# Four value products moved to later visits, a bias tile padded from 16 to 64 columns, four decay sums moved one block on

## The chip, the core and the metric

One core of a Trainium2 chip runs one launch of the kernel. The metric is the device time of a run in microseconds. The kernel before took 982.14, 982.09 and 980.04 us in three runs, so its median is 982.09 us.

## The reference, cut to what matters

Two layers on a sequence of 256 tokens with a model width of 2048. The first is a Mamba-2 mixer (8 groups, 64 heads of 64), the second a sliding-window attention with 32 query heads in 4 groups of 8, each group on one key/value head. Each layer ends in a layer norm. The part that the change touches most is the attention of one group and its output projection:

```python
s = jnp.einsum("bcqhrd,bckhd->bchrqk", qb, kk).astype(jnp.float32) * (hd ** -0.5)
s = jnp.where(valid[None, :, None, None], s, -jnp.inf)
...
p = jnp.exp(s - m)
p = p / (jnp.sum(p, axis=-1, keepdims=True) + jnp.exp(sk - m))
o = jnp.einsum("bchrqk,bckhd->bcqhrd", p.astype(vv.dtype), vv)
...
o = o * jax.nn.silu(gate)
return o @ w_out
```

In the Mamba layer, each head needs a 128 x 128 decay factor per chunk, the exponential of a difference of running sums, which the kernel makes on ScalarE.

## The kernel before, in words

**Products.** Every large matrix is kept in two halves: a rounded high part (`wh`, `xH`, `yH`, `x1H`, `oH`) and the rest (`wl`, `xL`, `yL`, `x1L`, `oL`), and each product is three matmuls, high by high, low by high and high by low. Weights arrive in units of 128 x 2048 numbers (two DMAs of 512 KB on the SP queue into `wr`). ScalarE makes the high half (L164), VectorE the low one (L167), two units ahead of their use. A unit then feeds TensorE in one of two forms:
- 48 matmuls of 128 x 256 (L252, in `mac`), with the weights stationary and the activations moving: the input projections of the first layer (`xH`, `xL`), and the query and gate projections of the second (`x1H`, `x1L`).
- 24 matmuls of 128 x 512 (L323 to L325, in `out_unit`), with the activations stationary and the weights moving: the output projections, from `yH`, `yL` in the first layer and from `oH`, `oL` in the second. The kernel has 8 groups of them in the first layer and 4 in the second.

**Visits.** Between units, TensorE makes short visits to small plain float32 products, which write PSUM tiles named `ax`: in the first layer the chunk products, in the second the scores (L1160 for the first 128 tokens, L1167 for the second) and the value products (L1270 for the first 128 tokens; L1284 and L1291 for the second).

**The second layer's clock.** The order of its units is `B_ORDER`: q0 g0 q1 g1 q2 o0 g2 q3 o1 g3 o2, each of four units, and o3 at the very end by `out_last`. A call to `tick()` stands behind every unit. `later(n, fn)` puts a piece of work into a list, and the n-th tick from there runs it; within a tick, pieces run in the order in which they were put in. For group j, `attend(j, 0)` (scores and softmax of the first half) runs three ticks behind the last query unit; it puts in `pv` of that half `PV_AT[j][0]` ticks on, and `attend(j, 1)` three ticks on, which puts in its own `pv` `PV_AT[j][1]` ticks on. `pv` multiplies by the values on TensorE, gates the result into `o` on VectorE (L1258), and splits it into `oH` (ScalarE, L1298) and `oL` (VectorE, L1299). Instructions of an engine stand in the order that the tile framework gives them; an engine runs them in that order.

**Tiles in memory.** The second layer's tiles come from the pool `bp`, laid one behind another in the order in which their tags first appear: `snk` (64 columns of 4 bytes), `rot`, `kT`, `vt`, `qT`, `qb`, and behind `qb` the tags `pt0`, `pri`, `gb0`, `gb1`, `qt`, `rt`, `p`, `sg`, `sm`, `own`, `ze`, `oH`, `oL` and some small ones. `qb` has 16 columns of 4 bytes, 64 bytes; every tile ahead of it has a multiple of 256 bytes. So in the built program `kT`, `vt` and `qT` start on a multiple of 256 bytes, and everything behind `qb`, `oH` (byte 161600) and `oL` (169792) among it, starts 64 bytes past one. The weight tiles, `yH`, `yL`, `x1H` and `x1L` start on multiples of 256. A unit of the query and gate projections lies 64 bytes into its weight tile (`BROKEN`), one of the output projections at its start (`WHOLE`).

**The first group.** `sum_decay(0, 0, ...)` makes the eight ScalarE instructions of the first half group's decay sums (L550), in two parts of four. They read `rb`, a copy of running sums that are written to memory and read back by a DMA. The first part is planned behind block 5 of the first layer (`halves[0][0]`), the second behind block 6. `beside[k]` instead puts a function into block k's convolution (`conv_silu`, L492 to L500), behind its ScalarE and VectorE scaling and ahead of its tanh.

Of the kernel before, what the change touches and what calls it, by code (L numbers as in the profile page):

```python
# [8 lines left out]
F32 = mybir.dt.float32  # L9
# [5 lines left out]
ALU = mybir.AluOpType  # L15
AX = mybir.AxisListType

P = 128
# [43 lines left out]

MOVE_AT = [[2, 3, 3, 4], [3, 4, 5, 6]]
MOVE_LAST = [2, 3, 3, 4]
PV_AT = [[6, 7], [6, 7], [8, 7], [7, 5]]
RES_AT = [2, 2, 3, 3, 4, 5, 5, 6]
ALPHA = (2.0 * 2) ** 0.25
NEG = -1.0e30
# [15 lines left out]
def trunk(ctx: ExitStack, tc: tile.TileContext, A: dict, out: bass.AP, dbg=None):  # L84
    nc = tc.nc
    PSUM = bass.MemoryType.PSUM

    def pool(name, bufs=1, side=None, space=None, stack=ctx):
        kw = {"space": space} if space is not None else {}
        return stack.enter_context(  # L90
            tc.tile_pool(name=name, bufs=bufs, side=side, reuse_waits="tile", **kw)
        )
# [165 lines left out]
    def later(n, fn, place=None):  # L258
        pending.insert(len(pending) if place is None else place, [n, fn])
# [562 lines left out]
    beside = {}  # L822
# [6 lines left out]
    def at(t, fn, *a):  # L829
        plan.setdefault(t, []).append((fn, *a))  # L830
# [5 lines left out]
    for g in range(NG):  # L836
        t = 10 * g
        if g == 0:
            at(TD, turn_dt, *dts)
            at(4, load_decay, 0, 1)  # L840
            at(8, load_low, 0)
            pos = dict(cb=CB0, y=13)

            between[11] = [(turn_first, 0)]
            halves = [(5, 6, 7), (7, 8, 9)]
            by = (9, 10)
        elif g == 1:
            at(10, load_decay, 1, 0)
            at(10, load_decay, 1, 1)
            at(15, load_low, 1)  # L850
            pos = dict(cb=6, y=Y_AT, norm=10 + CB_AT)

            halves = [(13, 14, 15), (15, 16, 16)]
            by = (16, 17)
        else:
            at(t - 5, load_decay, g, 0)
            at(t - 5, load_decay, g, 1)
            at(t, load_low, g)
            pos = dict(cb=CB_AT, y=Y_AT, norm=10 + CB_AT)
        for hf in range(2):  # L860
            if g < 2:
                sa, sb, ex = halves[hf]
                if (g, hf) != (1, 0):
                    at(sa, sum_decay, g, hf, 0, 2)
                at(sb, sum_decay, g, hf, 2, 4)
                at(ex, exp_decay, g, hf)
            else:
                for i in range(2):
                    beside[t + 3 * hf + i] = sum_decay, g, hf, 2 * i, 2 * i + 2
                beside[t + 3 * hf + 2] = exp_decay, g, hf  # L870
        if g == 1:
            at(16, norm, 0)
        at(t + pos["cb"], cb, g)
        for hf in range(2):
            at(by[hf] if g < 2 else t + pos["cb"] + hf, by_cb, g, hf)
        if g > 0:
            xs_at = t + 6
            if g == 1:
                between[17] = [(turn_xs, 1)]
            else:  # L880
                at(xs_at, turn_xs, g)
            for n, js in enumerate(((0, 1), (2, 3))):
                at(xs_at + n + (g == 1), carry_xs, g, js)
            at(xs_at + 2, scale_xs, g)
        at(t + pos["y"], ymm, g)
        if g == 0:
            at(t + pos["y"], sum_decay, 1, 0, 0, 2)
        for i in range(4):
            at(t + pos["y"], gate, g, i)
        if g > 0:  # L890
            at(t + pos["norm"], norm, g)
# [88 lines left out]
    bp = pool("bp")  # L980
# [56 lines left out]
    vt = bp.tile([P, 2, S], F32, tag="vt", name="vt")  # L1037
    kvb = bp.tile([P, 512], F32, tag="qT", name="kvb", bufs=2)
    nc.gpsimd.dma_start(kvb[:], A["kvb"].partition_broadcast(P))
    qb = bp.tile([P, 16], F32, tag="qb", name="qb")  # L1040
    nc.gpsimd.dma_start(qb[:], A["qb"])
    kv_u = []
    for h in range(2):
        ps = mm_tile()
# [36 lines left out]

    def rope_maps():

        nc.gpsimd.tensor_scalar(qb[:], qb[:], 0.125, None, ALU.mult)
        z = bp.tile([P, 2, 2, 32], F32, tag="rt", name="z", bufs=1)
        nc.vector.transpose(z[:].rearrange("p h m t -> p (h m t)"), turned[:].rearrange("p h m t -> p (h m t)"))
        for k in range(2):
            lo = 64 * k
            for a in range(4):
                nc.scalar.copy(  # L1090
                    rot[lo : lo + 32].rearrange("p m (h a t) -> p a m h t", h=2, a=4)[:, a],
                    z[32 * a : 32 * a + 32].rearrange("p h m t -> p m h t"),
                )

    later(1, rope_maps)
    swap = [*range(8, 16), *range(8), *range(16, 32)]

# [42 lines left out]
    def attend(j, h):  # L1140
# [161 lines left out]
        turn_far()  # L1302
        later(PV_AT[j][h], pv)
        if h == 0:
# [202 lines left out]
```

## Time and profile before

| what | value |
|---|---|
| three runs | 982.14, 982.09, 980.04 us |
| the profiled execution's own time | 980.68 us |
| its span, first to last instruction | 978.6 us |
| outside the span | 980.68 - 978.6 = 2.1 us |
| granted TensorE clock, mean | 0.999 |
| first layer, roughly | 0 to 651 us |
| second layer, roughly | 651 us to the end; query, gate and output units from 680 us |

The profile's page lists busy time per engine, then the chain of work that ended last, then groups of instructions. A group's row reads: line, engine, operation, output<-inputs, shapes, count, then busy us, mean ns of one, and the idle time ahead of them. In a timeline row the first column is the start, the second the length, both in us. A matmul's length is partly modelled and matmuls overlap, so the pace of a stream is the distance of starts, not the length. In the chain, a row is start, length, and what ran; "x144" says that 144 instructions are in it.

### The profile page before, as it was taken

Reading aid. Unit: us, or ns where it says so; the run is one execution under the profiler, and the core shown is the slowest. Engines: PE = TensorE matmul, PEld = TensorE weight load, DVE = VectorE, ACT = ScalarE, POOL = GpSimd, SP = SyncE. Lnnn points to the kernel's source line nnn. Section 1 sums busy time; section 2 is a strip of 40 time slices with the busy share of each in tenths; the row PEclk is TensorE's granted clock in tenths of the full one; section 3 lists DMA queues with packets and bytes.
Section 4 is the critical chain, followed back from the end, with each engine's and each line's share of the span. In section 5 each row is a group of like instructions: output and inputs, shape, how many; then the busy total and the mean of one; then the engine's idle time right before and its main releaser. Section 6 shows DMA issues by size and latency. Waiting matters only on the chain.

```text
span 978.6 us, 18818 instructions
## 1 busy us (share of the span) xinstructions
PE 972.5 (99%) x7364; PEld 896.7 (92%) x7364; DVE 789.4 (81%) x1202; ACT 666.5 (68%) x1254; POOL 103.2 (11%) x145
## 2 busy tenths in 40 slices
PE   9999999999999999999999999999999999999997
PEld 8999989999999998999999999888999988988976
DVE  7888898976888877885887787889977778778786
ACT  7585885864985865776576487467567776784762
POOL 0000303004003001200300300412000000000003
PEclk9999999999999999999999999999999999999999
DMA  9788567755665766666666566458654645465632
GB/s 357 251 284 326 160 210 235 249 201 152 207 218 190 250 208 199 212 200 206 191 205 201 171 211 198 148 187 272 200 159 144 195 153 191 141 208 170 218 127 87
DMA packets 61274, 197.91 MB, mean 202 GB/s; under 512 B 6801, under 2 KB 11329, under 8 KB 60929
## 3 DMA queue, kind: packets, MB, share of 16 engines
q1 hardware_dynamic: 58528, 188.53, 58.5%
q0 software_dynamic: 2048, 7.65, 2.5%
q8 instruction: 58, 0.95, 0.4%
q10 hardware_dynamic: 608, 0.52, 0.2%
q14 instruction: 32, 0.25, 0.1%
HBM read 194.45 MB, written 2.23 MB: 201 GB/s over the span
## 4 chain that ended last, share of the span: by engine, by line
PE 90%; DVE 5%; ACT 2%; issue 1%; DMA 1%; DVEq 0%; ACTq 0%
PE mm L252 56%; PE mm L323 9%; PE mm L324 9%; PE mm L325 9%; PE mm L1011 2%; PE ax L654 2%; DVE wl L167 1%; ACT e L550 1%; DVE cv L494 1%; DMA rb<-rscr 1%; PE ax L1167 1%; DMA wr<-in_wa 1%; ACT wh L164 1%; PE ax L1160 0%; PE mm L390 0%
## 5 line engine op out<-in xcount | busy, mean ns | idle before, releaser
L167 DVE TENSOR_TENSOR wl<-wr,wh 128x1024 fp32r<-128x1024 f32 (+2 forms) x354 | 394.2, 1133 | 80.1 <-ACT wh L164 76.9
L164 ACT ACTIVATE wh<-wr 128x1024 fp32r<-128x1024 f32 (+2 forms) x354 | 333.3, 974 | 104.6 <-PE mm L252 65.9
L252 PE MATMUL mm<-xH,wh 128*128 128x256 f32 x1280 | 354.7, 277 | 0.1
L252 PE MATMUL mm<-xH,wl 128*128 128x256 f32 x1280 | 353.9, 276 | 0.0
L252 PE MATMUL mm<-xL,wh 128*128 128x256 f32 x1280 | 353.9, 276 | 0.0
L252 PEld LDWEIGHTS mm<-xH,wh 128*128 128x128 f32 x1280 | 240.4, 188 | 2.3 <-issue 0.9
L252 PEld LDWEIGHTS mm<-xL,wh 128*128 128x128 f32 x1280 | 240.4, 188 | 1.0
L252 PEld LDWEIGHTS mm<-xH,wl 128*128 128x128 f32 x1280 | 240.3, 188 | 0.0
L252 PE MATMUL mm<-x1H,wh 128*128 128x256 f32 x512 | 143.0, 279 | 0.0
L252 PE MATMUL mm<-x1L,wh 128*128 128x256 f32 x512 | 141.8, 277 | 0.0
L252 PE MATMUL mm<-x1H,wl 128*128 128x256 f32 x512 | 141.7, 277 | 0.0
L323 PE MATMUL mm<-wh,yH 128*128 128x512 f32 x256 | 101.3, 396 | 0.1
L324 PE MATMUL mm<-wh,yL 128*128 128x512 f32 x256 | 99.8, 390 | 0.0
L325 PE MATMUL mm<-wl,yH 128*128 128x512 f32 x256 | 99.7, 389 | 0.0
L252 PEld LDWEIGHTS mm<-x1H,wh 128*128 128x128 f32 x512 | 96.1, 188 | 3.9 <-issue 2.4
L252 PEld LDWEIGHTS mm<-x1L,wh 128*128 128x128 f32 x512 | 96.4, 188 | 0.1
L252 PEld LDWEIGHTS mm<-x1H,wl 128*128 128x128 f32 x512 | 96.2, 188 | 0.0
L670 POOL TENSOR_TENSOR yz<-yz,z 128x256 f32<-128x256 f32 x32 | 26.8, 848 | 451.9 <-DVE yz L665 451.9
L494 DVE SCALAR_TENSOR_TENSOR cv<-mm,pc,cv 128x255 f32<-128x255 f32 x144 | 68.7, 478 | 5.2 <-ACT cv L492 2.6
L323 PEld LDWEIGHTS mm<-wh,yH 128*128 128x128 f32 x256 | 48.1, 188 | 10.6 <-DVE z L584 1.1
L325 PEld LDWEIGHTS mm<-wl,yH 128*128 128x128 f32 x256 | 48.1, 188 | 10.1
L324 PEld LDWEIGHTS mm<-wh,yL 128*128 128x128 f32 x256 | 48.1, 188 | 9.1
(235 smaller groups left out, 1246.6 us busy)
## 6 DMA issues: line engine op xcount, KB each, us to landing
wr<-in_wa SPq DMA_DIRECT2D x154, 512.0 KB, 5.2
wr<-in_wo SPq DMA_DIRECT2D x64, 512.0 KB, 4.6
wr<-in_wq SPq DMA_DIRECT2D x32, 512.0 KB, 4.5
wr<-in_wg SPq DMA_DIRECT2D x31, 512.0 KB, 4.5
wr<-in_wb SPq DMA_DIRECT2D x16, 512.0 KB, 4.7
wr<-in_wb SPq DMA_DIRECT2D x32, 256.0 KB, 3.7
rb<-rscr SPq DMA_DIRECT2D x11, 512.0 KB, 6.0
wr<-in_wkv SPq DMA_DIRECT2D x8, 512.0 KB, 5.6
```

The lines of the kernel that those rows point to most:

```text
L164: m = nc.scalar.activation(h[:, sl], v, AF.Copy)
L167: m = nc.vector.tensor_tensor(l[:, sl], v, h[:, sl].bitcast(F32), ALU.subtract)
L252: m = nc.tensor.matmul(ps, a, b, start=first and i == 0, stop=last and i == 2)
L323: pinned(nc.tensor.matmul(ps, aH[:, k, hs], u.h[:, ks], start=k == 0 and add is None, stop=False), pin)
L324: pinned(nc.tensor.matmul(ps, aL[:, k, hs], u.h[:, ks], start=False, stop=False), pin)
L325: pinned(nc.tensor.matmul(ps, aH[:, k, hs], u.l[:, ks], start=False, stop=k == 3), pin)
L494: nc.vector.scalar_tensor_tensor(a[:, sft:], ps[:, : S - sft], w(3 - sft), a[:, sft:], ALU.mult, ALU.add)
L550: m = nc.scalar.activation(e[:, h, cols], rb[:, h, c * P :], AF.Relu, scale=-1.0, bias=rtk[:, c, h0 + h : h0 + h + 1])
L654: nc.tensor.matmul(ps[64 * r : 64 * r + 64, cols], st.xd[:, c, i, 64 * r : 64 * r + 64], e[:, 256:] if c else e[:, :256], start=c == 0, st ...
L670: nc.gpsimd.tensor_tensor(v, v, st.z[i][:], ALU.mult)
L1011: m = nc.tensor.matmul(ps[:], (x1H, x1L, x1H)[i][:, kk, hs], (u.h, u.h, u.l)[i][:, ks], start=(kk, i) == (0, 0), stop=ui == 3 and (k, i) = ...
L1167: nc.tensor.matmul(pss[par][qs, at : at + 192], q2(rows, b + i, 64 * part, 64), kT[rows, j, 64 * part : 64 * part + 192], start=True, stop ...
```

## The change

Three things change. `PV_AT` gives the first half's `pv` two ticks more in groups 0, 1 and 2 and one tick more in group 3. `qb` is allocated with 64 columns, of which 16 are used. The first part of `sum_decay(0, 0, ...)` goes from the plan behind block 5 into `beside[3]`, the convolution of the block that runs as number 6.

```diff
-PV_AT = [[6, 7], [6, 7], [8, 7], [7, 5]]
+PV_AT = [[8, 7], [8, 7], [10, 7], [8, 5]]
...
                 sa, sb, ex = halves[hf]
-                if (g, hf) != (1, 0):
+                if (g, hf) == (0, 0):
+                    beside[3] = sum_decay, 0, 0, 0, 2
+                elif (g, hf) != (1, 0):
                     at(sa, sum_decay, g, hf, 0, 2)
...
-    qb = bp.tile([P, 16], F32, tag="qb", name="qb")
-    nc.gpsimd.dma_start(qb[:], A["qb"])
+    qb = bp.tile([P, 64], F32, tag="qb", name="qb")[:, :16]
+    nc.gpsimd.dma_start(qb, A["qb"])
...
-        nc.gpsimd.tensor_scalar(qb[:], qb[:], 0.125, None, ALU.mult)
+        nc.gpsimd.tensor_scalar(qb, qb, 0.125, None, ALU.mult)
```

With the ticks counted from the first query unit, the first half's `pv` goes from tick 13 to 15 (group 0), from 21 to 23 (group 1), from 31 to 33 (group 2) and from 42 to 43 (group 3). `attend(1, 0)` runs at tick 15, `attend(2, 0)` at 23, and the second half's `pv` of groups 2 and 3 at 33 and 43, all of them put in later than the moved piece and so behind it. The new padding is 192 bytes: every tile behind `qb` moves by that, and `oH` starts at byte 161792, `oL` at 169984, multiples of 256. The changed file is two lines longer, so that L1270 of before is L1272 there, L1258 is L1260, L1299 is L1301.

TensorE at tick 13, before: `pt` is the turned probabilities of the first half, `x1H`/`x1L` with `wh`/`wl` a gate unit.

```order
L252 MATMUL mm_8957<-x1H,wh_8813 128x256
L252 MATMUL mm_8957<-x1L,wh_8813 128x256
L252 MATMUL mm_8957<-x1H,wl_8814 128x256
L1270 MATMUL ax_9009<-pt_8547,vt 64x512 x2
L252 MATMUL mm_9034<-x1H,wh_8877 128x256
L252 MATMUL mm_9034<-x1L,wh_8877 128x256
L252 MATMUL mm_9034<-x1H,wl_8878 128x256
```

TensorE at tick 15, after; the L1162 rows are the scores of `attend(1, 0)`, which go on for six rows more, and then the next gate unit follows.

```order
L252 MATMUL mm_9093<-x1H,wh_8945 128x256
L252 MATMUL mm_9093<-x1L,wh_8945 128x256
L252 MATMUL mm_9093<-x1H,wl_8946 128x256
L1272 MATMUL ax_9145<-pt_8547,vt 64x512 x2
L1162 MATMUL ax_9157<-kT,qT_8681 128x128
L1162 MATMUL ax_9158<-kT,qT_8681 128x128
```

The value product has gone two units on and now stands directly ahead of the scores, so that one visit holds both. The same happens in group 1 ahead of the scores of group 2, and in groups 2 and 3 ahead of the second half's value products.

VectorE around the last value products, before. L334 adds an output product into the residual, L167 splits weights, L1258 gates, L1299 makes `oL`.

```order
L334 TENSOR_TENSOR xr<-xr,mm_11026 128x512
L1258 TENSOR_TENSOR o_11042<-ax_11043,sg_10629 128x512
L167 TENSOR_TENSOR wl_11110<-wr_11111,wh_11109 128x1024
L167 TENSOR_TENSOR wl_11110<-wr_11114,wh_11109 128x1024
L1299 TENSOR_TENSOR oL_11041<-o_11042,oH_11040 128x4x128
L334 TENSOR_TENSOR xr<-xr,mm_11066 128x512
L334 TENSOR_TENSOR xr<-xr,mm_11080 128x512
L167 TENSOR_TENSOR wl_11165<-wr_11166,wh_11164 128x1024
L1258 TENSOR_TENSOR o_11094<-ax_11095,sg_10629 128x4x64
```

VectorE at the same place, after.

```order
L334 TENSOR_TENSOR xr<-xr,mm_11071 128x512
L167 TENSOR_TENSOR wl_11165<-wr_11166,wh_11164 128x1024
L1260 TENSOR_TENSOR o_11087<-ax_11088,sg_10629 128x512
L167 TENSOR_TENSOR wl_11165<-wr_11169,wh_11164 128x1024
L1301 TENSOR_TENSOR oL_11086<-o_11087,oH_11085 128x4x128
L1260 TENSOR_TENSOR o_11094<-ax_11095,sg_10629 128x4x64
L1260 TENSOR_TENSOR o_11094<-ax_11096,sg_10629 128x4x64
L334 TENSOR_TENSOR xr<-xr,mm_11121 128x512
L1301 TENSOR_TENSOR oL_11086<-o_11094,oH_11085 128x4x128
```

The gating and the low half of the first 128 tokens have gone one unit on, behind both residual adds of that unit and the next weight split.

ScalarE in the first group, before: L550 are decay sums, L499 a convolution's tanh, L164 a weight split.

```order
L477 ACTIVATE f_441<-rtk 128x128
L550 ACTIVATE e_727<-rb_509,rtk 128x256
L550 ACTIVATE e_727<-rb_509,rtk 128x128
L550 ACTIVATE e_727<-rb_509,rtk 128x256
L499 ACTIVATE ct_643<-cv_644 128x256
L550 ACTIVATE e_727<-rb_509,rtk 128x128
L164 ACTIVATE wh_732<-wr_736 128x1024
L164 ACTIVATE wh_803<-wr_805 128x1024
L499 ACTIVATE xs_712<-cv_713 128x256
L492 ACTIVATE cv_792<-mm_742,pc 128x256
```

ScalarE at the same place, after.

```order
L477 ACTIVATE f_441<-rtk 128x128
L164 ACTIVATE wh_727<-wr_731 128x1024
L499 ACTIVATE ct_643<-cv_644 128x256
L164 ACTIVATE wh_803<-wr_805 128x1024
L164 ACTIVATE wh_803<-wr_807 128x1024
L499 ACTIVATE xs_712<-cv_713 128x256
L492 ACTIVATE cv_787<-mm_737,pc 128x256
L550 ACTIVATE e_792<-rb_509,rtk 128x256
L550 ACTIVATE e_792<-rb_509,rtk 128x128
L550 ACTIVATE e_792<-rb_509,rtk 128x256
```

Three weight splits and two tanhs now stand ahead of the four decay sums. The order of the SP and the POOL queues is the same in both kernels.

## The prediction

> **What bounds the kernel now.** I read the page's busy table and chain first.
>
> ```profile
> PE 972.5 (99%) x7364; PEld 896.7 (92%) x7364; DVE 789.4 (81%) x1202; ACT 666.5 (68%) x1254; POOL 103.2 (11%) x145
> PE 90%; DVE 5%; ACT 2%; issue 1%; DMA 1%; DVEq 0%; ACTq 0%
> ```
>
> TensorE is busy for 972.5 us, 99% of the span, and holds 90% of the chain. Such a busy time can hide slow matmuls, since their ends are modelled. So the question is at which pace the matmuls start, and what it costs to go from a stream to a visit and back. I looked at both in the timeline of TensorE, for output units of the first layer (first and last of 24 rows of L323) and of the second (first and last of 15).
>
> ```profile
> 634.78 0.39 PE L323 MATMUL mm<-wh,yH 128*128 128x512 f32 x1
> ...
> 650.43 0.39 PE L323 MATMUL mm<-wh,yH 128*128 128x512 f32 x1
> ```
>
> ```profile
> 806.63 0.39 PE L323 MATMUL mm<-wh,oH 128*128 128x512 f32 x1
> ...
> 816.43 0.39 PE L323 MATMUL mm<-wh,oH 128*128 128x512 f32 x1
> ```
>
> Each L323 stands for three matmuls. First layer: 15.65 us / (23 x 3) = 226.8 ns from start to start. Second layer: 9.80 / (14 x 3) = 233.3 ns. Nothing waits in either stretch; the units are alike in shape, count and weight buffers, and the one operand that differs is the stationary one: `yH`/`yL` start on a multiple of 256 bytes, `oH`/`oL` 64 bytes past one. The groups by form show it in the lengths as well:
>
> ```profile
> L324 PE MATMUL mm<-wh,yL 128*128 128x512 f32 x256 | 99.8, 390 | 0.0
> L324 PE MATMUL mm<-wh,oL 128*128 128x512 f32 x124 | 49.0, 395 | 0.0
> ```
>
> **Term 1, the padding: -2.5 us.** The 192 bytes put `oH` and `oL` on multiples of 256, as `yH` and `yL` are; the moving weights stay where they are. The row of `oL` counts 124 matmuls of 512 columns, and each product is three of them: 372. If all take the first layer's pace, that is 372 x (233.3 - 226.8) = 2.4 to 2.5 us; I take 2.5. The 24 matmuls of 256 columns at the end I leave alone. From above the term is bound by a row in which equal residues look bad: the first product of a unit of the first layer, whose `xH` piece and weights both start on a multiple of 256.
>
> ```profile
> 200.45 0.29 PE L252 MATMUL mm<-xH,wh 128*128 128x256 f32 x1
> 200.57 0.28 PE L252 MATMUL mm<-xL,wh 128*128 128x256 f32 x1
> ...
> 201.04 0.28 PE L252 MATMUL mm<-xH,wl 128*128 128x256 f32 x1
> 201.15 0.28 PE L252 MATMUL mm<-xH,wh 128*128 128x256 f32 x1
> ```
>
> There the starts are 120 ns apart at first and 113 later, 6% more. 6% on 226.8 ns would be 240.4 ns, so the term lies between -2.5 and 372 x 7.1 = +2.6 us. I take the lower end: its row has the same shape, the same weights and the same residues as the changed product.
>
> [...]
>
> **Term 2, four visits fewer: -0.8 us.** A lone visit of the first half's value products:
>
> ```profile
> 754.45 0.28 PE L252 MATMUL mm<-x1H,wl 128*128 128x256 f32 x1
> 754.66 1.08 PE L1270 MATMUL ax<-pt,vt 128*64 128x512 f32 x4
> 755.67 0.39 PE L252 MATMUL mm<-x1H,wh 128*128 128x256 f32 x1
> 755.89 0.28 PE L252 MATMUL mm<-x1L,wh 128*128 128x256 f32 x1
> ```
>
> From the last stream matmul to the visit it is 0.21 us instead of 0.113, and from the first stream matmul behind it to the second 0.22: two edges of 0.10 and 0.11, together 0.2 us. Inside the visit, 1.01 us stay, wherever it stands: in the chain, L1284 has the same number of columns (8 x 256 against 4 x 512) and takes the same 1.01 us with another float32 product behind it.
>
> ```profile
> 779.08 1.01 PE ax L1284 x8
> 780.09 0.59 PE ax L1291 x8
> 780.68 5.85 PE mm L252 x48
> ...
> 787.99 11.31 PE mm L252 x96
> ...
> 831.25 5.85 PE mm L252 x48
> ```
>
> So each merge saves the two edges, 4 x 0.2 = 0.8 us. It is 0.5 if the seam costs what it does elsewhere: L591 takes 0.43 us behind a stream and 0.52 behind L694.
>
> ```profile
> 58.85 0.59 PE L591 MATMUL ax<-ct,bt 128*128 128x256 f32 x2
> 59.28 0.38 PE L592 MATMUL ax<-ct,bt 128*128 128x128 f32 x2
> ```
>
> ```profile
> 107.28 0.68 PE L591 MATMUL ax<-ct,bt 128*128 128x256 f32 x2
> 107.80 0.38 PE L592 MATMUL ax<-ct,bt 128*128 128x128 f32 x2
> ```
>
> Nothing waits for the moved results: group 0's outputs are first used at tick 21 and are now ready behind tick 17, group 1's by 25 against 33, group 2's by 33 against 41. A merged visit needs three of the four `ax` tiles. The tight place is group 3, whose `oL` of the first half was made here, well ahead of o3, which begins one unit later:
>
> ```profile
> 942.09 0.68 DVE L1299 TENSOR_TENSOR oL<-o,oH 128x512 fp32r<-128x512 f32 x1
> ```
>
> Counted from the start of the merged visit, VectorE now does a residual add and then waits for a new `wh` half (about 1.4 us), a split (2.35 for two in a row quoted below, so 1.2), the gating (0.68, as `oL`), a split (1.2) and `oL` (0.68): ready at about 5.2 us. TensorE needs 1.01 + 1.01 + 0.59 us for the visit and 24 x 0.227 = 5.4 us for the last unit of o2 before the next layer of products, 8.1 us. About 3 us are spare, so this costs nothing; if VectorE came 3 us late, each further microsecond would go straight to the end.
>
> **Term 3, the pace behind visits: 0.** The units at 780.68 and 831.25, each behind L1291, take 5.85 us; of that 0.2 are edges, and 5.65 / 48 is 118 ns from start to start, against 113 to 114 in the rows of term 1 (a unit of 5.45). The pair at 787.99, behind L1167 two ticks later, has 11.31 - 10.9 - 0.1 (its one edge) = 0.3 too much; the same visit one group on is followed by such a unit too. That is some 0.9 us in all. The products are the same ones after the change; the visits ahead of them (`ptw`, `pte`, and `qT` of odd groups) move by 192 bytes, which may start the stream another way. I take 0, with -0.9 and +0.9 as ends.
>
> **Term 4, the decay sums: 0.** ScalarE stands still for a DMA, and VectorE behind it:
>
> ```profile
> ACT e L550 <- DMA rb<-rscr: 2.6, 1, 2.6
> ```
>
> ```profile
> 50.97 0.43 DVE L500 SCALAR_TENSOR_TENSOR ct<-ct,cv 128x256 f32<-128x256 f32 x1 [2.36 <-ACT ct L499]
> ...
> 51.70 2.35 DVE L167 TENSOR_TENSOR wl<-wr,wh 128x1024 fp32r<-128x1024 f32 x2
> ```
>
> ```profile
> 53.64 0.28 PE L252 MATMUL mm<-xH,wl 128*128 128x256 f32 x1
> ```
>
> The first of those two splits ends near 52.9, TensorE uses it at 53.64: 0.7 us to spare, so the 2.6 us were hidden, and in this execution nothing is won. Where `rb` lands over 0.7 us later, TensorE would have waited, and no longer does. TensorE's only later waits for engines in that layer stand at 130 and 136 us:
>
> ```profile
> 130.17 0.19 PEld L323 LDWEIGHTS mm<-wh,yH 128*128 128x128 f32 x1 [0.27 <-DVE z L584]
> 135.99 0.19 PEld L252 LDWEIGHTS mm<-xH,wh 128*128 128x128 f32 x1 [0.51 <-issue]
> ```
>
> ```profile
> 100.00:110.00 10.00, 10.00 (x80) 9.62 (x79) 9.56 (x12) 5.24 (x10) 6.26 (x8) 1.00 0.48 130
> 110.00:120.00 10.00, 10.00 (x70) 9.21 (x69) 6.13 (x19) 10.00 (x19) 1.12 (x2) 1.00 0.57 195
> ```
>
> The windows (PE, PEld, DVE, ACT busy) show ScalarE half idle until 110 us and full afterwards, so that backlog is made later than the moved work. Ends: -0.8 (both waits gone, 0.27 + 0.51) and +0.8 (both doubled).
>
> **Sum.** -2.5 - 0.8 + 0 + 0 = -3.3 us on the profiled execution's own 980.68 us (span 978.6 and 2.1 around it): 977.4. The median of the runs, 982.09, is 1.4 above that execution, and the same sum from it gives 978.8. Part of that spread may be late `rb` copies, which the change takes off the path, so I lean to the first and say 977.9.
>
> **Rivals.**
> - *The padding does nothing*: something else slows the output units of the second layer. For it: the rows of before show no kernel with the same tiles at another address. Against it: no wait stands in either stretch, and shape, weights and order are the same. Only term 2 is left: 977.9 + 2.5 = 980.4. [...]
> - *Slower: equal residues are the bad case, as in the first product of a unit.* Place: the 372 output matmuls. Price: 240.4 ns each, +2.6 - 0.8 = +1.8 us, 982.5 from the profiled execution and 983.9 from the median. It makes the kernel slower from a pace of 233.3 + 800/372 = 235.5 ns on. Against it: 768 first-layer matmuls with equal residues at 226.8 ns.
> - *A new wait*: the later gating of group 3 (or a late PSUM tile at a merged visit) holds TensorE. It needs 3 us of delay before it costs anything, and 6 before it eats the gain: about 980.5 to 982.
> - *More than forecast*: the four 118 ns units return to 113, and the waits at 130 us go: -0.9 - 0.8 more, 976.2.
>
> **How the numbers follow.** The forecast case gets 0.76, the idle padding 0.10, equal residues 0.04, a new wait 0.04, more than forecast 0.06. The forecast's own range is 977.9 with terms 2 and 3 (-0.9 to +1.2) and a microsecond of spread between runs, about 976.0 to 980.0. 975.6 to 980.2 takes in the last rival and leaves out the three others, 0.18 in all. A measurement of this kernel can tell about 0.2%, 2 us, from no change. Faster by more: 0.76 + 0.06 + a little of the rest = 0.83; within 0.2%: 0.13; slower: 0.04.
>
> **What would show it.** Term 1: L323 to L325 with `oH`, `oL` at 227 ns from start to start, lengths near 390. Term 2: no lone L1272 between stream units, four edges of 0.2 us fewer. Term 3: which units behind L1293 and L1169 run at 118 ns. Term 4: no wait of the decay sums for `rb`, and the same TensorE starts up to 120 us. The forecast is wrong if output units stay at 233 ns, or if TensorE waits for `oL` near 945 us.

## The result and the profile after

The changed kernel took 979.57 us in the median of 20 runs (978.67 to 981.89), the kernel before, beside it, 981.46 (979.32 to 983.62). The ratio is 0.9985, with a 95% interval of 0.9979 to 0.9991: faster by 0.9 to 2.1 us. The forecast had -3.3 from the profiled execution. So the sign was right and the forecast size about twice the measured one.

The profiled execution took 978.68 us, 2.0 less than that of before. Busy time and chain of the changed kernel:

```profile
PE 969.5 (99%) x7364; PEld 896.4 (92%) x7364; DVE 789.3 (81%) x1202; ACT 666.9 (68%) x1254; POOL 101.3 (10%) x145
PE 92%; DVE 3%; ACT 2%; issue 1%; DMA 1%; SPq 0%; DVEq 0%; ACTq 0%
```

TensorE is still 99% busy. What changed is read from starts. I compare the first matmul of the first query unit with the first of the last four products of o3, first in the kernel before, then in the changed one.

```profile
679.82 0.28 PE L252 MATMUL mm<-x1H,wh 128*128 128x256 f32 x1
...
968.34 0.28 PE L323 MATMUL mm<-wh,oH 128*128 128x256 f32 x1
```

```profile
679.22 0.28 PE L252 MATMUL mm<-x1H,wh 128*128 128x256 f32 x1
...
966.14 0.28 PE L323 MATMUL mm<-wh,oH 128*128 128x256 f32 x1
```

The second layer takes 286.9 us instead of 288.5: **-1.6 us**. That is the ratio's -1.5. The other 0.6 us, gained ahead of 679 us, turned out to be chance (e3 and e10, below). So did the 0.2 us lost behind o3: e3, which changes nothing there, loses 0.4. So the second layer is where the change has to be explained, and there are two gains and three losses in it.

**The pace** is what was forecast. A stretch of output products without a wait, and the row of the group, in the changed kernel:

```profile
812.24 0.39 PE L323 MATMUL mm<-wh,oH 128*128 128x512 f32 x1
...
814.96 0.39 PE L323 MATMUL mm<-wh,oH 128*128 128x512 f32 x1
```

```profile
L324 PE MATMUL mm<-wh,oL 128*128 128x512 f32 x124 | 48.5, 391 | 0.0
```

2.72 us for 4 x 3 matmuls is 226.7 ns. **The merged visits** are there too. The first one, TensorE in the changed kernel:

```profile
764.96 0.28 PE L252 MATMUL mm<-x1H,wl 128*128 128x256 f32 x1
765.17 1.08 PE L1272 MATMUL ax<-pt,vt 128*64 128x512 f32 x4
766.18 1.16 PE L1162 MATMUL ax<-kT,qT 64*128 64x128 f32 x16
767.27 0.39 PE L252 MATMUL mm<-x1H,wh 128*128 128x256 f32 x1
```

The scores follow the value products after 1.01 us, with no stream between. **The losses** are three waits that before did not have. The first is at the start of group 0's third output unit, its fifth product (the expectations below call it the second unit): TensorE's weight load, then VectorE's queue ahead of what it waits for.

```profile
810.04 0.19 PEld L323 LDWEIGHTS mm<-wh,oH 128*128 128x128 f32 x1 [0.89 <-DVE xr L330]
```

```profile
807.52 0.67 DVE L1225 TENSOR_TENSOR z<-z,cc 128x512 f32<-128x512 f32 x1
808.11 0.68 DVE L1123 TENSOR_TENSOR qT<-qT,rot 128x512 f32<-128x512 f32 x1
808.72 0.68 DVE L1123 TENSOR_TENSOR sw<-sw,rot 128x512 f32<-128x512 f32 x1
809.32 0.68 DVE L330 SCALAR_TENSOR_TENSOR xr<-xr,mm 128x512 f32<-128x512 f32 x1
```

This L330 reads group 0's first product out of its PSUM tile. There are four `mm` tiles, so the fifth product needs that tile again and cannot start before L330 is done. L330 stands behind a mask product and rotary products of other work. I count from group 0's first output product, in the kernel before (with its L330) and in the changed one:

```profile
799.14 0.39 PE L323 MATMUL mm<-wh,oH 128*128 128x512 f32 x1
808.90 0.67 DVE L330 SCALAR_TENSOR_TENSOR xr<-xr,mm 128x512 f32<-128x512 f32 x1
```

```profile
798.51 0.40 PE L323 MATMUL mm<-wh,oH 128*128 128x512 f32 x1
```

Before, L330 begins at 9.76 us and TensorE wants the tile at 12.39. In the changed kernel L330 begins at 10.81 us, and TensorE wants the tile at 10.9 us (as in e8 and e12, where it does not wait), since the pace is faster and the lone visit of group 1 is gone. So VectorE has become 1.05 us later as well. That goes with the move of group 0's value product: L330 begins at 9.7 to 9.9 us in the six kernels that leave it in its place (before, e1, e3 to e6) and at 10.8 to 11.0 us in the five that move it and leave VectorE's queue here as it is (the changed kernel, e2, e7, e10, e11). The moved gating and `oL` now stand in VectorE's queue where group 1's softmax begins. The wait costs 0.8 us: to the unit behind the next scores it is 19.33 us from the first output product, 18.54 in e8 and e12.

The second wait is inside a visit, the scores of group 2's second half, which take 1.85 us:

```profile
836.45 1.85 PE L1169 MATMUL ax<-kT,qT 64*64 64x192 f32 x32
```

In the kernel before the same visit takes 1.53:

```profile
837.03 1.53 PE L1167 MATMUL ax<-kT,qT 64*64 64x192 f32 x32
```

The third is the one that the prediction named and priced at nothing: the `oL` of group 3, TensorE's weight load in the changed kernel, and VectorE's queue from the start of the merged visit at 936.79 us.

```profile
945.51 0.19 PEld L324 LDWEIGHTS mm<-wh,oL 128*128 128x128 f32 x1 [0.72 <-DVE oL L1301]
```

```profile
937.85 0.68 DVE L334 TENSOR_TENSOR xr<-xr,mm 128x512 f32<-128x512 f32 x1
938.44 2.35 DVE L167 TENSOR_TENSOR wl<-wr,wh 128x1024 fp32r<-128x1024 f32 x2
940.71 1.28 DVE L334 TENSOR_TENSOR xr<-xr,mm 128x512 f32<-128x512 f32 x2
941.91 1.22 DVE L167 TENSOR_TENSOR wl<-wr,wh 128x1024 fp32r<-128x1024 f32 x1
943.05 0.68 DVE L1260 TENSOR_TENSOR o<-ax,sg 128x512 f32<-128x512 f32 x1
943.65 1.21 DVE L167 TENSOR_TENSOR wl<-wr,wh 128x1024 fp32r<-128x1024 f32 x1
944.78 0.68 DVE L1301 TENSOR_TENSOR oL<-o,oH 128x512 fp32r<-128x512 f32 x1
```

`oL` is ready 945.46 - 936.79 = 8.7 us after the visit began, not 5.2. VectorE had a residual add, two splits and another residual add to do before the residual add at which the prediction's count begins; the wait for `wh` that the count has in it did not come.

### The profile page after: what moved, and what is told of

Read it like the earlier page. It is cut to its first block, busy times and chain, and to the rows that moved or that the text cites. A ratio compares the mean times of both kernels' runs of the same rounds, so it can differ in the third digit from the quotient of the medians.

```text
span 976.6 us, 18816 instructions
## 1 busy us (share of the span) xinstructions
PE 969.5 (99%) x7364; PEld 896.4 (92%) x7364; DVE 789.3 (81%) x1202; ACT 666.9 (68%) x1254; POOL 101.3 (10%) x145
## 4 chain that ended last, share of the span: by engine, by line
PE 92%; DVE 3%; ACT 2%; issue 1%; DMA 1%; SPq 0%; DVEq 0%; ACTq 0%
PE mm L252 61%; PE mm L323 8%; PE mm L324 8%; PE mm L325 8%; PE ax L654 2%; PE mm L1013 2%; DVE wl L167 1%; DMA first<-in_first 1%; PE ax L1169 0%; PE ax L1162 0%; PE ax L591 0%; ACT p L1197 0%; DVE z L1211 0%; ACT ptw L1230 0%; ACT pt L1230 0%
## 5 line engine op out<-in xcount | busy, mean ns | idle before, releaser
L167 DVE TENSOR_TENSOR wl<-wr,wh 128x1024 fp32r<-128x1024 f32 (+2 forms) x354 | 393.8, 1132 | 81.4 <-ACT wh L164 78.7
L164 ACT ACTIVATE wh<-wr 128x1024 fp32r<-128x1024 f32 (+2 forms) x354 | 333.6, 974 | 107.2 <-PE mm L252 66.7
```

The lines of the kernel that those rows point to most:

```text
L164: m = nc.scalar.activation(h[:, sl], v, AF.Copy)
L167: m = nc.vector.tensor_tensor(l[:, sl], v, h[:, sl].bitcast(F32), ALU.subtract)
```

## The experiments

Waits that come by chance in the first layer (up to 1.8 us of TensorE's time, e10 below) hide differences of this size. So each kernel is given twice: its ratio to the kernel before, from the runs, and the length of its second layer against before (first query unit to the last products of o3), from one trace. The second layer is the same program in before and e3, and in the changed kernel and e10; these pairs agree within 0.04 us.

| kernel | ratio, 95% interval | second layer, us |
|---|---|---|
| changed kernel | 0.9985 (0.9979 to 0.9991) | -1.59 |
| e1 padding alone | 0.9987 (0.9979 to 0.9996) | -1.36 |
| e2 value products alone | 0.9995 (0.9987 to 1.0004) | -0.50 |
| e3 decay sums alone | 0.9997 (0.9985 to 1.0009) | 0.00 |
| e4 tile of 32 columns | one run, 980.75 us | -0.32 |
| e5 tile of 48 columns | one run, 979.78 us | -1.08 |
| e6 weights 64 bytes in | one run, 979.62 us | -1.81 |
| e7 groups 1 and 3 put back | 0.9988 (0.9976 to 0.9999) | -1.11 |
| e8 residual adds first | 0.9986 (0.9977 to 0.9995) | -1.83 |
| e9 rotary on GpSimd | 1.0000 (0.9991 to 1.0008) | -0.03 |
| e10 early load | 0.9987 (0.9973 to 1.0002) | -1.55 |
| e11 early load, group 3 put back | 0.9980 (0.9971 to 0.9989) | -1.73 |
| e12 short rotary | one run, 980.61 us | -1.41 |

My theory at the start: the pace and the merges are worth what was forecast, and the waits that take half of it back come from VectorE being late. The rivals were that the pace itself is worth less, that the two profiles differ by chance, and that the waits have other causes.

**e1, the padding alone.** The kernel before, with this, and the two uses of `qb` as in the change:

```diff
-    qb = bp.tile([P, 16], F32, tag="qb", name="qb")
+    qb = bp.tile([P, 64], F32, tag="qb", name="qb")[:, :16]
```

> The kernel before with the wide bias tile alone: the instructions and their order on every engine are those of before, and only addresses differ. Theory: the pace of the second layer's 372 output products of 512 columns is set by where the stationary tile starts, so they go from 233.3 to about 227 ns from start to start and the time falls by 2.2 to 2.8 us (ratio 0.9972 to 0.9978). The waits that the changed kernel has near 809, 837 and 945 us are not here. Rival: most of the gain is taken by new waits that a faster stream itself causes (VectorE and the weights come later against TensorE), so the pace is 227 ns but the time falls by 1.5 us or less (ratio 0.9985 or more).

The pace went to 227 ns, the time fell by 0.0013 x 981 = 1.3 us: the rival. The output units give 2.1 us by the trace, and two things take back: the unit behind L1071 at 697 us runs 0.2 us slower (as in every kernel here with the 64-column tile, and in none with 16, 32 or 48), and the scores of group 2's second half now wait, 0.7 us. The unit behind these scores gives 0.2 us back; it takes 5.56 us instead of 5.76. TensorE in e1:

```profile
838.04 1.20 PE L1167 MATMUL ax<-kT,qT 64*64 64x192 f32 x16 [0.18 <-DVE o L1258]
```

That row starts 1.06 us behind the first sixteen of the visit, at 836.98; the unit behind them begins 0.73 us later against the unit ahead than in the kernel before. So the wait near 837 us comes with the faster output units alone. The waits near 809 and 945 us are not in e1.

**e2, the value products alone.** The kernel before, with this:

```diff
-PV_AT = [[6, 7], [6, 7], [8, 7], [7, 5]]
+PV_AT = [[8, 7], [8, 7], [10, 7], [8, 5]]
```

> The kernel before with the four value products moved, tile and decay sums as before. Theory: four merged visits save 4 edges of 0.2 us and some 0.15 us more in two of them, about 1.1 us, and the new waits at the first output unit of group 0, in the scores of the second half of group 2 and for the oL of group 3 cost about 1.5 us, so the time rises by 0.4 us, with a spread of -0.3 to +0.9 (ratio 0.9997 to 1.0009). Rival: the new waits come from the faster output units and not from the moved products; then they are absent here and the time falls by 0.8 to 1.1 us (ratio 0.9989 to 0.9992).

-0.5 us both ways, between the two; the interval of the runs includes 1, so the trace decides. By TensorE's starts the merges save 0.21 us (group 0), 0.36 (group 2) and 0.33 (group 3; 0.39 in the kernels with the wide tile). The wait near 809 us is here, in one stretch with the merge of group 1, and the two together cost 0.43 us. What that merge is worth shows where it stands without the wait: e8 and e12 take 18.54 us from the first output product of group 0 to the unit behind the next scores, e7, which puts the merge back, 18.77. So it saves 0.2 us, as in group 0, and the wait alone costs 0.6 us here. Since it is not in e1, it comes from the move. No wait for `oL` is here: that one needs the move and the faster units together.

**e3, the decay sums alone.**

```diff
-                if (g, hf) != (1, 0):
+                if (g, hf) == (0, 0):
+                    beside[3] = sum_decay, 0, 0, 0, 2
+                elif (g, hf) != (1, 0):
```

> The kernel before with the four decay sums moved alone. Theory: the waits at 130 and 136 us of before go, as they did in the changed kernel, and the time falls by 0.7 us (ratio about 0.9993); the units from 124 to 141 us take 5.45 to 5.55 us each. Rival: those waits differ from run to run with the start of the first loads, and have nothing to do with the moved sums; then they stand here as in before, and the ratio is 1.0000.

The rival holds. The interval of the runs has room for both, 1.0000 and the theory's 0.9993; the traces decide. The two waits at 130 and 136 us are gone in e3, but just as much in e1, e2, e4, e5 and e6, whose sums stand where they stood; they were an accident of that one profile of before. In e8, whose sums are moved, TensorE takes 0.84 us more than in the changed kernel between 125 and 140 us. The wait of the sums for `rb` is gone, and ScalarE waits for weights in its place, between 36 and 140 us of e3:

```profile
ACT wh L164 <- DMA wr<-in_wa: 3.7, 3, 1.7
```

In e6 the wait for `rb` is 4.5 us instead of 2.6, and yet TensorE takes the same time from 42 to 144 us as in e3, within 0.05:

```profile
ACT e L552 <- DMA rb<-rscr: 4.5, 1, 4.5
```

**e4, e5, e6: what sets the pace.** e4 and e5 are e1 with 32 and 48 columns. e6 leaves the tile and moves the weights of the second layer's output units:

```diff
+        if what == "o":
+            places.update({len(srcs) + i: [[(16, 0, KT)], [(16, 0, KT)]] for i in range(4)})
```

> The kernel before with a bias tile of 32 columns, so that oH and oL start 128 bytes past a multiple of 256 and the weights on one; order as before. Theory: an output product runs at 227 ns only where both operands have the same start in a multiple of 256, so the units stay at 233 ns or more here. Rival: 64 bytes apart is the one bad case, and the units go to 227 ns.

> The kernel before with a bias tile of 48 columns, so that oH and oL start 192 bytes past a multiple of 256 and the weights on one; order as before. Theory: 227 ns only with equal starts, so 233 ns or more here. Rival: 227 ns, as only 64 bytes apart is bad.

> The kernel before, with oH and oL left 64 bytes past a multiple of 256, and the weights of the second layer's output projections put 64 bytes into their tiles as well. The order on every engine is that of before. Theory: the pace is set by where the stationary tile starts, by itself; then the output units of the second layer stay at 233 ns from start to start (5.60 us a unit). Rival: it is set by the difference between the start of the stationary and the moving tile; then they go to 227 ns (5.45 us a unit), as in the changed kernel.

The mean distance of starts over the 512-column products (357 distances in each trace; those over 300 ns, waits and first products behind a visit, are left out):

| start of `oH`, `oL` past 256 | start of the weights | ns |
|---|---|---|
| 64 bytes (before) | 0 | 233.2 |
| 0 (changed kernel, and e1) | 0 | 227.5 |
| 128 (e4) | 0 | 232.5 |
| 192 (e5) | 0 | 229.0 |
| 64 (e6) | 64 | 227.4 |

e6 tells it: nothing was aligned there, only made equal, and the pace is that of the changed kernel. In these five cases the pace goes with the difference of the two starts, as the rival had it. Weights at 64 bytes were tried with one start of `oH` alone, and whether 256 is the period was not tried. It is also no matter of good and bad: 192 bytes apart costs 1.5 ns, 64 apart 5.7, so that e4 comes out near the theory's 233 and e5 as neither side said. The groups' mean lengths (395 ns before, 391 in the changed kernel) go roughly the same way, in e6, e4 and e5, though e5's does not stand apart:

```profile
L326 PE MATMUL mm<-wh,oL 128*128 128x512 f32 x124 | 48.3, 389 | 0.0
```

```profile
L324 PE MATMUL mm<-wh,oL 128*128 128x512 f32 x124 | 48.9, 394 | 0.0
```

```profile
L324 PE MATMUL mm<-wh,oL 128*128 128x512 f32 x124 | 48.5, 391 | 0.0
```

e6 has the order of before on every engine, and its second layer is 0.2 us shorter than that of the changed kernel. So equal starts alone, without the wide tile, give as much as the whole change. Beside the padding alone (e1) the moved value products, with the waits that they bring, add 0.2 us.

**e7, two value products put back.** The changed kernel, with this:

```diff
-PV_AT = [[8, 7], [8, 7], [10, 7], [8, 5]]
+PV_AT = [[8, 7], [6, 7], [10, 7], [7, 5]]
```

> The changed kernel with the first half's value products of groups 1 and 3 where they stood before; those of groups 0 and 2 stay in the merged visits. Theory: the lone visits come back (0.2 us in group 1, 0.35 us in group 3) and the waits at the first output unit of group 0 (0.65 us) and for the oL of group 3 (0.58 us) go, so the time is 0.7 us below the changed kernel, about 2.2 us below before (ratio 0.9978). Rival: the waits stay, since VectorE is late at these places by its other work; then the time is 0.5 us above the changed kernel, 1.0 us below before (ratio 0.9990).

Half wrong. The waits near 809 and 945 us are gone, as expected, and yet the second layer is 0.5 us longer than in the changed kernel. The wait in the scores near 837 us has grown to 1.04 us, TensorE in e7:

```profile
840.15 1.21 PE L1169 MATMUL ax<-kT,qT 64*64 64x192 f32 x16 [1.04 <-DVE o L1260]
```

It waits for the gating of the value products one visit earlier, which still hold two of the four `ax` tiles. In sums: two merges lost, 0.2 and 0.4 us; two waits spared, 0.8 and 0.6; the scores 1.3 us longer; together +0.5. So the waits at 809 and 837 us are not two prices that can be struck off one by one: time that TensorE does not lose at the first it loses at the second.

**e8, the residual adds first.** The changed kernel, with this:

```diff
-            nc.vector.scalar_tensor_tensor(v, v, ALPHA, ps, ALU.mult, ALU.add)
+            with tc.high_priority(200): nc.vector.scalar_tensor_tensor(v, v, ALPHA, ps, ALU.mult, ALU.add)
```

> The changed kernel, with the residual adds of group 0's output units put ahead of other VectorE work in its queue (the first one goes ahead of one mask product and two rotary products, 2 us). Theory: VectorE is full from 801 to 828 us, so whatever goes first makes another thing late; the 0.5 us wait at group 0's second output unit goes, and the wait in the scores near 837 us grows from 0.3 us by about as much; the time is within 0.3 us of the changed kernel (ratio to before 0.9983 to 0.9989). Rival: only the order was bad; the wait goes, nothing takes its place, and the time is 0.5 us below the changed kernel (ratio about 0.9980).

The wait near 809 us is gone, and the one near 837 us is 0.70 us:

```profile
839.07 1.21 PE L1169 MATMUL ax<-kT,qT 64*64 64x192 f32 x16 [0.70 <-DVE o L1260]
```

From the first query unit to the unit behind these scores e8 is 0.15 us longer than the changed kernel, so this is the theory's side: what one is spared the other takes. (The whole second layer is 0.24 shorter, since `oL` near 945 us happened to be less late.)

**e9, rotary products on GpSimd.** The changed kernel, with this, and the sum behind it likewise:

```diff
-                    nc.vector.tensor_tensor(
+                    (nc.gpsimd if j == 2 else nc.vector).tensor_tensor(
                         v[:], v[:], rot[:, m : m + 1, :].to_broadcast([P, 2, S]), ALU.mult
```

> The changed kernel, with the six rotary products and sums of group 2's queries on GpSimd instead of VectorE. This takes 6 x 0.68 = 4.1 us out of VectorE's queue between 790 and 811 us. Theory: VectorE is what holds TensorE between 801 and 838 us; with the room, the waits at group 0's second output unit (0.5 us) and in the scores near 837 us (0.3 us) go, and the second layer is 0.8 us shorter than in the changed kernel (ratio to before about 0.9977). Rival: these waits come from other things (the order of VectorE's queue, ScalarE's exponentials), so they stay, or GpSimd's products of some 1.3 us each make the scores of group 2 late; the time is that of the changed kernel or more.

It lost the whole gain. TensorE waits 1.42 us at the same product as in the changed kernel:

```profile
811.51 0.50 PE L323 MATMUL mm<-wh,oH 128*128 128x512 f32 x1 [1.42 <-DVE xr L330]
```

Two reasons are in VectorE's queue of e9. With the rotary products gone, a weight split took their place ahead of L330. And some of its instructions that run beside GpSimd's products are slower: that split takes 2.33 us and those at 793.28 and 811.38 us 2.04 and 1.69, 1.2 elsewhere, and L1192 takes 1.05, 0.17 elsewhere. VectorE, then the products of GpSimd:

```profile
796.83 1.05 DVE L1192 TENSOR_TENSOR sm<-sm,snk 128x8 f32<-128x8 f32 x1
...
808.53 2.33 DVE L167 TENSOR_TENSOR wl<-wr,wh 128x1024 fp32r<-128x1024 f32 x1
810.78 0.67 DVE L330 SCALAR_TENSOR_TENSOR xr<-xr,mm 128x512 f32<-128x512 f32 x1
```

```profile
794.20 2.28 POOL L1123 TENSOR_TENSOR sw<-sw,rot 128x512 f32<-128x512 f32 x1
796.56 1.30 POOL L1126 TENSOR_TENSOR qT<-qT,sw 128x512 f32<-128x512 f32 x1
808.13 1.65 POOL L1123 TENSOR_TENSOR qT<-qT,rot 128x512 f32<-128x512 f32 x1 [10.27 <-DVE sw L1121]
```

GpSimd's own six products take between 1.30 and 2.28 us. So e9 does not tell whether VectorE's load is the cause. e12 does.

**e12, less work for VectorE and none in its place.** The changed kernel, with the rotary products of group 2 on 64 of each 256 columns, and the sum likewise. The kernel leaves out the rest of the rotary embedding for that group.

```diff
-                        v[:], v[:], rot[:, m : m + 1, :].to_broadcast([P, 2, S]), ALU.mult
+                        v[:, :, : 64 if j == 2 else S], v[:, :, : 64 if j == 2 else S],
+                        rot[:, m : m + 1, : 64 if j == 2 else S].to_broadcast([P, 2, 64 if j == 2 else S]), ALU.mult
```

> The changed kernel with the rotary products of group 2's queries made on 64 of each 256 columns alone; it leaves out the rest of the rotary embedding for that group. This takes about 6 x 0.43 = 2.6 us out of VectorE between 790 and 811 us with no work for GpSimd in its place. Theory: VectorE's work in that stretch is what holds TensorE; the waits at group 0's second output unit (0.5 us) and in the scores near 837 us (0.3 us) go, so that the start of the second unit of g2 stands 0.8 us earlier, against the start of the second layer, than in the changed kernel. Rival: VectorE's lateness is made by its waits for ScalarE's exponentials, whatever it does ahead of them; then the wait near 837 us stays or grows, as it did where the residual adds were put forward.

The theory falls in this form. The wait at 809 us is gone, and the one near 837 us is 0.73 us, as large as in e8:

```profile
839.05 1.21 PE L1171 MATMUL ax<-kT,qT 64*64 64x192 f32 x16 [0.73 <-DVE o L1262]
```

What VectorE won it lost again waiting for ScalarE's halves of the weights, 2.8 us between 805 and 830 us of e12, 0.5 in the changed kernel and in e8:

```profile
DVE wl L167 <- ACT wh L164: 2.8, 4, 1.4
```

In the kernel before VectorE has no such wait in that stretch, but one of 1.1 us for ScalarE's `oH`. The windows of e12 (PE, PEld, DVE, ACT busy) show why:

```profile
810.00:815.00 5.00, 5.00 (x23) 4.14 (x23) 4.17 (x6) 4.89 (x12) 0.00 (x0) 1.00 0.54 170
815.00:820.00 5.00, 5.00 (x33) 3.29 (x33) 3.05 (x6) 4.89 (x12) 0.00 (x0) 1.00 0.74 261
```

ScalarE is full from 810 to 820 us: it copies the turned probabilities into `ptw` and `pte`, 0.4 us each, and makes the weight halves in between. VectorE comes free earlier and waits for it. Behind that comes a wait of 2.6 us for ScalarE's exponentials, near 832 us, which is the same in all fourteen profiles. So in this stretch, between q2 and the scores at 837 us, two engines run one behind the other, and TensorE runs against both. How the lateness divides between the weight halves and the exponentials no run tells.

This was so before. The gating that frees the tile for the scores, and the first matmul of the unit behind them, in before and in e12:

```profile
836.89 0.74 DVE L1258 TENSOR_TENSOR o<-ax,sg 128x256 f32<-128x256 f32 x2
838.49 0.39 PE L252 MATMUL mm<-x1H,wh 128*128 128x256 f32 x1
```

```profile
838.58 0.75 DVE L1262 TENSOR_TENSOR o<-ax,sg 128x256 f32<-128x256 f32 x2
840.18 0.39 PE L252 MATMUL mm<-x1H,wh 128*128 128x256 f32 x1
```

From the end of the gating to that matmul it is 0.86 us in both, and 0.86 to 0.89 in all fourteen profiles. Before, the scores just need not wait; wherever TensorE gained something ahead of them, they do. So the matmul stands 158.6 to 159.2 us behind the first query unit in twelve of the profiles (159.7 in e7, 160.6 in e9), whatever was done ahead of it. The changed kernel loses 0.35 us up to there, 159.02 us against 158.67, and gains 1.95 behind it.

**e10, the small load earlier.** The difference of the profiles ahead of 679 us led to one row. VectorE waits near 239 us for `inv`, a load of 8 columns on GpSimd's queue, and the wait differs from run to run. In e7:

```profile
241.19 0.36 DVE L803 TENSOR_SCALAR ang<-inv,posf 128x8 f32<-128x8 f32 x2 [1.78 <-DMA inv<-in_inv]
```

In the other profiles it was 0.27 (before), none (changed kernel), 1.07 (e1), 1.30 (e2), 0.90 (e3), 0.88 (e4), none (e5), 0.28 (e6), 0.18 (e8), 0.51 (e9) and 1.56 (e12). Between 258 and 286 us TensorE took, against the changed kernel, 1.82 us more in e7, and in the others in this order 0.05, 0, 0.88, 1.42, 0.93, 0.93, 0, 0.34, 0, 0.31 and 1.46 us more. VectorE does not catch up in between (against the changed kernel, e7's L803 begins 2.31 us later and its first L332 behind 269 us 2.30 later), and TensorE pays 30 us later. e10 is the changed kernel with the load issued earlier (`load_inv` holds the load that stood in `rotary`):

```diff
+    at(26, load_inv)
     at(38, rotary)
```

> The changed kernel, with the small load of inv issued 70 us earlier on GpSimd's queue; everything else stands as it did. In six profiles VectorE waits for that load near 239 us for 0 to 1.8 us, and TensorE loses 0 to 1.8 us near 269 us. Theory: the first is the cause of the second and makes most of the spread between runs; without it no run loses there, the median falls by 0.4 to 0.8 us below the changed kernel and the runs lie closer together (ratio to before 0.9977 to 0.9982). Rival: VectorE's lateness at 269 us has another cause, the loss near 269 us stays, and the time is that of the changed kernel (ratio 0.9985).

VectorE finds `inv` there (no wait in the row), and TensorE loses nothing near 269 us:

```profile
238.87 0.36 DVE L805 TENSOR_SCALAR ang<-inv,posf 128x8 f32<-128x8 f32 x2
```

The median is 979.22 us, 0.35 below the changed kernel's, but the kernel before had 981.10 beside it and not 981.46, so that both lie 1.9 below before. The theory's ratio of 0.9977 to 0.9982 did not come: it is 0.9987, and the interval reaches from 0.9973 to 1.0002. One run of 986.09 us is in it, with a granted clock of 0.995. The other ten lie between 978.61 and 979.47, within 0.9 us, where the 20 runs of the changed kernel spread over 3.2. But e11, with the same early load, has nine runs from 978.08 to 979.10 and two at 980.70 and 980.82. So the traces show that the load makes TensorE lose up to 1.8 us in a run; that it makes most of the spread is not shown, and a gain in the median is not either.

**e11, group 3 put back as well.** e10, with this:

```diff
-PV_AT = [[8, 7], [8, 7], [10, 7], [8, 5]]
+PV_AT = [[8, 7], [8, 7], [10, 7], [7, 5]]
```

> The changed kernel with the small load of inv issued earlier, and the first half's value product of group 3 where it stood before; the merged visits of groups 0 to 2 stay. Theory: the merged visit of group 3 saves 0.33 us and its late oL costs 0.59, so without it the stretch from the second unit of o2 to the end is 0.25 us shorter than in the changed kernel, no wait for oL stands near 945 us, and the time is about 0.2 us below the kernel with the early load alone (ratio to before 0.9978 to 0.9986). Rival: the residual adds and splits that stand between are late either way, and the wait for oL only moves to a later unit; then it is 0.3 us above it.

As expected: no wait for `oL`, the second layer 0.18 us shorter than in e10, and 978.69 us in the median (978.08 to 980.82), ratio 0.9980. It has the lowest median of the study. That it beats before is shown. That it beats the change is not shown by the runs, since the intervals overlap; it rests on one trace of the second layer, -1.73 against -1.59.

## Why the prediction was half right

**Term 1, the pace: cause right, size off by a sixth.** The forecast -2.5 us (its own 372 x 6.5 ns is 2.4) came out as -2.1 over the output units of e1. The 226.8 ns came from an undisturbed stretch of the first layer; over all products of the second layer it is 227.5, since the first five distances behind a visit are 230 to 234 ns in the mean. 372 x 5.7 ns is 2.1 us. The two operands' starts matter to the pace, by e1 and e6: 227.5 and 227.4 against 233.2 ns at one shape, with nothing changed but addresses. What the hardware does there no run showed.

**Term 2, the merges: right in kind, too small.** Groups 0 and 1 saved the forecast 0.2 us each, 0.21 and 0.20. Groups 2 and 3 saved 0.36 and 0.39, since there the merged visit is itself 0.15 us shorter than its two parts: 2.47 us against 1.01 + 1.61. That is 1.2 us instead of 0.8. So terms 1 and 2 add up to the forecast -3.3 only because the two misses cancel, which is luck.

**Terms 3 and 4: right in the sum.** One unit became 0.2 us slower (behind L1071) and one 0.2 faster (behind the scores at 837 us); that they cancel is luck. The second is as fast in e2 and e6, where the visits' tiles lie where they lay, so the prediction's reason, that these tiles move, is not what makes it faster. The decay sums are worth 0.00 in e3. More was to spare there than the prediction's 0.7 us: in e6 the wait for `rb` is 1.9 us longer, and TensorE loses 0.05. My first reading of the two profiles, 0.7 us for them, was wrong, as e1, e2, e4, e5 and e6 showed.

**The step that failed is "Nothing waits for the moved results", with its "About 3 us are spare".** Three waits came in its place: 0.8 us at 809, 0.3 at 837 (0.1 with the faster unit behind it) and 0.6 at 945. Two are not for results at all, but for PSUM tiles that VectorE empties late. The prediction's working had asked only when results are needed; a late PSUM tile stood among the rivals alone, as one that costs nothing below 3 us of delay. Ahead of 838 us these two waits cost all that the faster pace and the merges gained there. The third was in the text with a wrong count: I began VectorE's queue at the rows that changed places and left out the splits and the residual adds that stood in it already, 8.7 us instead of 5.2. By the prediction's own sign, a wait for `oL` near 945 us, that part was wrong. -2.1 - 1.2 + 0.8 + 0.3 + 0.6 is -1.6, the second layer's -1.59. So the gains came out as forecast, and the waits, which were priced at nothing, took half of them. The measured time still lies in the stated range, which was wide enough for that.

The start was a little off as well: the median of three runs, 982.09, lay 0.6 above the 981.46 of twenty.

What stays open: why the pace goes with the two starts, and why the unit behind L1071 is slower with the wide tile. That ScalarE and VectorE together hold TensorE ahead of 838 us is read from the traces; a kernel in which both ScalarE and VectorE get room between 790 and 838 us was not tried.

## What to carry to other kernels

When a busy TensorE is made faster, ask at each stage which engine empties its PSUM tiles and how much slack that one has. Here VectorE had none near 837 us, and the stage's gain was given back in the next wait: with the wait at 809 us gone, the one in the scores near 837 us, 0.3 us in the changed kernel, was 0.70 in e8, 0.73 in e12 and 1.04 in e7. In the changed kernel all that TensorE gained ahead of that gating was lost, and the 1.95 us gained behind it stayed. Count a queue from the event on, with everything that stands in it already. Differences of a microsecond between two profiles are read from the stage that the change touches, and the rest is checked against profiles in which nothing was changed there.

## What was not expected of the hardware

- The pace of 128 x 128 x 512 products went with the difference of the operands' starting bytes: 227.5 and 227.4 ns with equal starts (both at 0, both at 64), 229.0, 232.5 and 233.2 at 192, 128 and 64 bytes apart.
- A load of 8 columns from GpSimd's queue, issued at the same point of the program, let VectorE wait between 0 and 1.8 us, and waits of 0.9 us and more cost TensorE about as much 30 us later.
- With GpSimd at work on 128 x 512 products, a VectorE instruction on 128 x 8 took 1.05 us instead of 0.17 and three weight splits 1.69 to 2.33 instead of 1.2, while the residual add at 810.78 us took 0.67 as elsewhere, and GpSimd's own products took up to 2.28 instead of 1.30.
